# A hybrid attention and convolution layer on one core: two helper constants built later, one weight tile loaded alone, and sums over partitions merged per head

## The chip, the core and the metric

The kernel runs on one core of one Trainium2 chip. The metric is the device time of one execution in microseconds (us), as the median of several runs; lower is better. Before the change the median of 3 runs is 643.99 us (642.95 to 644.54).

## What is computed

One layer with batch 1, 1024 positions and width 1024, all in float32:

```python
h = rms_norm(x, pre_norm_gain)
q, k, v, z_a, b_gate, c_gate, u, z_c = split(h @ w_in, 8)
# group A: 4 heads, two softmax maps each, block-causal mask, ALiBi
attn = (softmax(q0 k0' + bias) - lam * softmax(q1 k1' + bias)) @ v
attn = rms_norm(attn, subln_gain, 1e-5) * 0.2 * silu(z_a)
# group B: gated depthwise convolution of width 3
conv_out = b_gate * conv3(c_gate * u) * silu(z_c)
x = x + rms_norm(concat(attn, conv_out) @ w_out, post_norm_gain)
e = rms_norm(p @ w_ple_proj, ple_norm_gain)
out = x + sigmoid(x @ w_ple_gate) * e
```

## The kernel before

Everything stands transposed: features on the 128 partitions, positions along the row, in two halves of 512 (`n` = 0, 1). Every product is split into three matmuls (`mm3`, L99 to L102), since each float32 operand is held as a high part and a low part: L100 is high by high, L101 high by low, L102 low by high. The high part is a cast on ACT, the low part a subtraction on DVE or, for most weights, on POOL (`split`, L87 to L93). In the names, `pth`/`pto` are high and low part of p, `wph`/`wpo` those of `w_ple_proj`, `hT` those of x, `w` those of a weight tile.

The stages in order of time:

- **Start (0 to about 42 us).** Nine idle matmuls (L347), then the embedding p @ w_ple_proj (`embed`, L330 to L340): 8 tiles of 6 matmuls for each half. Its weights come in three loads into buffers of the pool `rawp`, which has three (`load_ple`, L303 to L318): tile 0 on ACT's queue (128 KB), tiles 1 to 3 with a table of small constants (402.5 KB), tiles 4 to 7 (512 KB), both on SP's queue; p comes in quarters (`load_p`, L320 to L328), x in 16 tiles (`load_x`, L298). DVE also builds two helpers out of the identity here (L170 to L172): `fold`, 128 by 128, in four reductions, and `own`, 128 by 4, in one. All later sums over partitions use them.
- **Projections.** `run` (L144) makes q, k and z of head 0, then v for all heads (L401), with the weights `wv`, whose four tiles are loaded at L395 and split on ACT and DVE.
- **Heads.** `PLAN` (L31) lists the steps of each head: softmax tiles (`a`), values (`g0`, `g1` for the halves, L256), convolution tiles to keep PE busy (`c`, 48 matmuls each), scaling the values by their norms (`n0`, `n1`, `scale_values` L283), and the embedding's norms (`s0`, `s1`, `embed_scale` L447).
- **Output.** The product with `w_out`, its norm, the product with `w_gate`, stores.

A sum of squares over partitions is `column_sums` (L105): DVE transposes 32 by 32 blocks (`flip`), reduces (`part`), PE multiplies by `fold` (a single matmul `ms`, L116, into a bank of 512), then `rsqrt` (L95) makes a scale on DVE and takes the power -0.5 on POOL (L97, 128 by 16), with the exponent from the constant `nhalf`. `values` does this once for each half of each head, with 16 columns of sums and 16 of softmax sums (`extra`, through `own`), `embed_scale` once for each half, and x and the output twice each: 14 `ms` matmuls and 14 powers in all.

The order of instructions on each engine is not written by hand. The program is scheduled as a whole by a timing model when it is built, so a change in one place can move rows in others; an engine then works through its rows strictly in that order, and SP's queue does so with the loads.

Of the kernel before, what the change touches and what calls it, by code (L numbers as in the profile page):

```python
# [43 lines left out]
def hybrid_layer(ctx, tc, xT, pT, w_in, lams, w_out, w_ple, w_gate, outT):  # L44
# [14 lines left out]
    small_c = edge.tile([P, 96], F32, name="small_c")  # L59
# [16 lines left out]
    nhalf = small_c[:, 4:20]  # L76
# [10 lines left out]
    def split(hi, lo, src, scale=None, lo_eng=None):  # L87
        if scale is None:
            A.copy(out=hi, in_=src)  # L89
            (lo_eng or V).tensor_tensor(out=lo, in0=src, in1=hi.bitcast(F32), op=sub)  # L90
# [14 lines left out]
    def column_sums(acc, pool, extra=None, tag="flip"):  # L105
        flip = pool.tile([P, HALF], F32, tag=tag, name="flip")
        V.transpose(out=flip, in_=acc)
        part = tiny.tile([P, 32], F32, tag="part", name="part")
        V.tensor_reduce(out=part[:, 0:16], in_=flip.rearrange("p (f r) -> p f r", r=32), axis=AX.X, op=add)
        if extra is not None:  # L110
            V.tensor_tensor(out=part[:, 16:32].rearrange("p (t f) -> p t f", t=4),
                            in0=extra.unsqueeze(2).broadcast_to([P, 4, 4]),
                            in1=own.unsqueeze(1).broadcast_to([P, 4, 4]), op=mult)
        n = 16 if extra is None else 32
        ms = bank_t("ms")
        T.matmul(out=ms[:, :n], lhsT=fold, rhs=part[:, :n], start=True, stop=True)  # L116
        return ms

# [33 lines left out]
    r_col = const.tile([P, NT + 80], F32, name="r_col")[:, :NT]  # L152
    R = [const.tile([P, HALF], F32, name=f"R{n}") for n in range(2)]

    with ExitStack() as st:
# [14 lines left out]
        for g in range(4):  # L170
            V.tensor_reduce(out=fold[:, 32 * g:32 * g + 32], in_=ident.rearrange("p (a b) -> p b a", a=4), axis=AX.X, op=add)
        V.tensor_reduce(out=own, in_=ident.rearrange("p (f r) -> p f r", r=32), axis=AX.X, op=add)  # L172

        class Head:
            def __init__(s, h):
# [12 lines left out]
                s.rs = {}  # L188
# [67 lines left out]
            def values(s, g):  # L256
# [16 lines left out]
                ms = column_sums(sq, ap, extra=r0)  # L273
                rb = tiny.tile([P, 16], F32, tag="rb", name="rb")
                rs = tiny.tile([P, 16], F32, tag="rs", name="rs")
                V.tensor_copy(out=rb, in_=ms[:, 16:32])
                V.tensor_tensor(out=rs, in0=ms[:, 0:16], in1=rb, op=mult)
# [3 lines left out]
                s.rs[g] = rs  # L281
# [8 lines left out]
        with ExitStack() as st0:  # L290
# [13 lines left out]
            def load_ple(c, o, queue=nc.sync, constants=0):  # L304
# [6 lines left out]
                cuts = [0, 1, c.stop - c.start] if constants else [0, c.stop - c.start]  # L311
                for a, b in zip(cuts, cuts[1:]):
                    w = slice(c.start + a, c.start + b)
                    if c.start == 0:
                        V.tensor_copy(out=wph[:, w], in_=raw[:, a:b])
                        V.tensor_tensor(out=wpo[:, w], in0=raw[:, a:b], in1=wph[:, w].bitcast(F32), op=sub)
                    else:
                        split(wph[:, w], wpo[:, w], raw[:, a:b])  # L318

            def load_p(n):  # L320
                pth = s2.tile([P, 2, HALF], F32R, tag="pth", name="pth")
                pto = s2.tile([P, 2, HALF], F32R, tag="pto", name="pto")
                raw = p_raw[:, n].bitcast(F32).rearrange("p (k a) b -> p k (a b)", k=2)
                for k in range(2):
                    nc.sync.dma_start(out=raw[:, k], in_=pT[:, n, k])
                    split(pth[:, k], pto[:, k], raw[:, k])
                return pth, pto

            def embed(n, p):
                pth, pto = p  # L330
# [20 lines left out]
            load_ple(slice(1, 4), 256, constants=37)  # L351
            load_ple(slice(4, 8), 1024 + 37)
            embed(0, pt0)
# [11 lines left out]
        with ExitStack() as st0:  # L365
# [81 lines left out]
        def embed_scale(n):  # L447
# [23 lines left out]
        for h in range(H):  # L471
# [5 lines left out]
            for step in PLAN[h]:  # L477
# [21 lines left out]
    with ExitStack() as st:  # L499
# [40 lines left out]
        def post_stat(n):  # L540
            r = tiny.tile([P, 16], F32, tag="rs", name="rso")
            rsqrt(r, column_sums(accs[n], cp)[:, :16], D, 1e-6)
# [90 lines left out]
```

## Time and profile before

| | before |
|---|---|
| median of 3 runs | 643.99 us |
| profiled execution, its own time | 643.39 us |
| its span, first to last instruction | 641.6 us |
| PE busy | 632.6 us, 99% |
| DVE busy | 447.9 us, 70% |
| ACT busy | 242.3 us, 38% |
| POOL busy | 227.6 us, 35% |
| mean granted TensorE clock | 0.996 |

PE is TensorE's matmuls, DVE the vector engine, ACT the scalar engine, POOL GpSimd, SP the engine that issues most loads and stores. A row of a timeline gives start and duration in us, the engine, the line of the kernel, what is written from what, and in brackets how long the engine stood idle before it and on whom it waited. Matmuls overlap in the pipeline: a matmul of 512 columns is listed with 0.39 us, but the next one starts 0.227 us later, so the pace of PE is read from the starts. The profiled execution lies 0.60 us under the median and inside the spread of the three runs.

### The profile page before, as it was taken

How to read it: one execution, taken by the hardware profiler on the slowest of the kernel's cores; microseconds unless marked ns; L12 is line 12 of the kernel's file. 1: busy time of each engine (PE TensorE's matmuls, PEld its weight loads, DVE VectorE, ACT ScalarE, POOL GpSimd, SP SyncE). 2: the span in 40 equal slices, each digit the busy share in tenths (PEclk: the TensorE clock that was granted, in tenths of full speed). 3: DMA queues.
4: the chain of work that ended last, by engine and by line, in shares of the span. 5: the costliest groups of instructions: out<-in, count | busy, mean ns of one | idle time of the engine just before them, and what ended most of it. 6: DMA issues, size and time to landing. Idle time of an engine off the chain costs nothing.

```text
span 641.6 us, 8064 instructions
## 1 busy us (share of the span) xinstructions
PE 632.6 (99%) x2941; PEld 524.8 (82%) x2941; DVE 447.9 (70%) x824; ACT 242.3 (38%) x442; POOL 227.6 (35%) x114
## 2 busy tenths in 40 slices
PE   8999999999999999999999999999999999999997
PEld 4888788888888888887888888888888888888886
DVE  6977612688786688776886999628993179898342
ACT  5936312334454333553343533322732225413111
POOL 2013300324326636237461142433760087741000
PEclk8999999999999999999999999999999999999999
DMA  8976612210244112353113411111360034124231
GB/s 301 391 268 161 228 78 102 88 39 27 83 130 149 50 33 59 85 170 97 36 33 90 127 46 34 42 55 36 119 242 33 2 98 150 64 84 146 84 114 50
DMA packets 35511, 67.78 MB, mean 106 GB/s; under 512 B 3600, under 2 KB 12304, under 8 KB 35472
## 3 DMA queue, kind: packets, MB, share of 16 engines
q1 hardware_dynamic: 35328, 67.14, 31.6%
q8 instruction: 23, 0.38, 0.2%
q10 hardware_dynamic: 144, 0.13, 0.1%
q14 instruction: 16, 0.13, 0.1%
HBM read 48.38 MB, written 12.58 MB: 95 GB/s over the span
## 4 chain that ended last, share of the span: by engine, by line
PE 89%; DVE 4%; DMA 3%; POOL 2%; ACT 1%; issue 1%; POOLq 0%; DVEq 0%; ACTq 0%
PE pj L100 13%; PE pj L102 13%; PE pj L101 13%; PE o L102 9%; PE o L100 9%; PE o L101 9%; PE s L237 5%; PE tpw L264 2%; PE v L100 2%; PE v L102 2%; PE v L101 2%; PE av L102 1%; PE ple L101 1%; PE av L101 1%; POOL mix L455 1%; PE av L100 1%
## 5 line engine op out<-in xcount | busy, mean ns | idle before, releaser
L100 PE MATMUL pj<-hT,w 128*128 128x512 f32 x448 | 176.3, 394 | 0.0
L101 PE MATMUL pj<-hT,w 128*128 128x512 f32 x448 | 176.2, 393 | 0.0
L102 PE MATMUL pj<-hT,w 128*128 128x512 f32 x448 | 176.2, 393 | 0.0
L90 POOL TENSOR_TENSOR w<-raw,w 128x1024 fp32r<-128x1024 f32 x41 | 105.6, 2581 | 145.1 <-ACT w L89 145.1
L102 PEld LDWEIGHTS pj<-hT,w 128*128 128x128 f32 x448 | 84.2, 188 | 16.4
L101 PEld LDWEIGHTS pj<-hT,w 128*128 128x128 f32 x448 | 84.2, 188 | 16.2
L100 PEld LDWEIGHTS pj<-hT,w 128*128 128x128 f32 x448 | 84.2, 188 | 16.1
L245 ACT ACTIVATE p<-p,nm 128x128 f32<-128x128 f32 (+7 forms) x64 | 49.4, 772 | 70.6 <-DVE nm L241 60.7
L89 ACT CAST w<-raw 128x1024 fp32r<-128x1024 f32 x44 | 45.8, 1047 | 19.4 <-issue 11.0
L102 PE MATMUL o<-x,w 128*128 128x512 f32 (+1 forms) x136 | 51.3, 377 | 0.0
L100 PE MATMUL o<-x,w 128*128 128x512 f32 (+1 forms) x136 | 51.2, 377 | 0.0
L101 PE MATMUL o<-x,w 128*128 128x512 f32 (+1 forms) x136 | 51.2, 377 | 0.0
L100 PE MATMUL o<-mT,w 128*128 128x512 f32 x128 | 49.8, 389 | 0.0
L101 PE MATMUL o<-mT,w 128*128 128x512 f32 x128 | 49.8, 389 | 0.0
L102 PE MATMUL o<-mT,w 128*128 128x512 f32 x128 | 49.7, 390 | 0.0
L237 PE MATMUL s<-ks,qs 128*128 128x512 f32 (+2 forms) x192 | 47.5, 346 | 0.5 <-ACT w L89 0.5
L89 ACT CAST wt<-tpw 128x512 fp32r<-128x512 f32 (+3 forms) x48 | 21.1, 479 | 60.2 <-PE tpw L264 60.2
L90 DVE TENSOR_TENSOR wt<-tpw,wt 128x512 fp32r<-128x512 f32 (+3 forms) x48 | 25.3, 550 | 26.3 <-ACT wt L89 26.2
L241 DVE CUSTOM_DVE_ANT_0 p<-s,bias 128x512 f32<-128x512 f32 (+3 forms) x64 | 34.8, 564 | 9.4 <-PE s L237 5.4
L237 PEld LDWEIGHTS s<-ks,qs 128*128 128x128 f32 x192 | 33.3, 188 | 5.8 <-ACT w L89 0.8
L418 POOL TENSOR_TENSOR mix<-mix,R 128x512 f32<-128x512 f32 x8 | 12.3, 1542 | 66.1 <-DVE mix L417 64.0
L253 DVE SCALAR_TENSOR_TENSOR p<-p,rl,p 128x128 f32<-128x128 f32 (+7 forms) x32 | 32.7, 1021 | 0.4
(142 smaller groups left out, 1101.6 us busy)
## 6 DMA issues: line engine op xcount, KB each, us to landing
raw<-in_w_in SPq DMA_DIRECT2D x32, 512.0 KB, 3.4
mix<-in_xT SPq DMA_DIRECT2D x16, 256.0 KB, 5.5
e_dram<-e SPq DMA_DIRECT2D x16, 256.0 KB, 6.0
mix<-e_dram SPq DMA_DIRECT2D x16, 256.0 KB, 3.0
ks<-ks SPq DMA_DIRECT2D x16, 256.0 KB, 3.6
v_dram<-v SPq DMA_DIRECT2D x8, 512.0 KB, 2.6
vs<-v_dram SPq DMA_DIRECT2D x32, 128.0 KB, 2.7
raw<-in_w_out SPq DMA_DIRECT2D x8, 512.0 KB, 3.3
```

The source lines that it names most:

```text
L89: A.copy(out=hi, in_=src)
L90: (lo_eng or V).tensor_tensor(out=lo, in0=src, in1=hi.bitcast(F32), op=sub)
L100: T.matmul(out=ps, lhsT=ah, rhs=bh, start=first, stop=False)
L101: T.matmul(out=ps, lhsT=ah, rhs=bl, start=False, stop=False)
L102: T.matmul(out=ps, lhsT=al, rhs=bh, start=False, stop=last)
L237: T.matmul(out=banks[m][:, :nn], lhsT=s.qs[:, m, qi], rhs=s.ks[:, m, part, c], start=part == 0, stop=part == 1)
L241: V.tensor_tensor_reduce(out=pr[m][:, c0:c0 + n], in0=banks[m][:, :n], in1=s.bias[:, b0:b0 + n], scale=-1.0, scalar=low[m], op0=add, op1=A ...
L245: A.activation(out=pr[m][:, :W], in_=pr[m][:, :W], func=AF.Exp, scale=-1.0, bias=low[m], accum_out=l[:, m:m + 1])
L253: V.scalar_tensor_tensor(out=pr[0][:, :W], in0=pr[1][:, :W], scalar=rl, in1=pr[0][:, :W], op0=mult, op1=add)
L264: T.transpose(out=tp[:, ii * P:(ii + 1) * P], in_=s.ws[ii][:, j * P:(j + 1) * P], identity=ident)
L418: G.tensor_tensor(out=o, in0=o, in1=R[n], op=mult)
L455: G.tensor_tensor(out=acc, in0=acc, in1=e, op=add)
```

## The change

Four things are changed. The five reductions that build `fold` and `own` are issued after the last low part of p's first half, not before. The load of tiles 1 to 3 is cut: tile 1 comes alone (128 KB) and is cast on DVE in place of ACT; tiles 2 and 3 come with the constants (274.5 KB). In each head, both halves put their sums into one tile of 64 columns, and a new step `r` (`row_scales`) makes one `ms` matmul, one chain of small DVE operations and one power of 32 columns, where each half had its own. The embedding's two halves likewise share one `ms` and one power of 32 columns, made in the second half's call. There are 9 `ms` matmuls and 9 powers now.

```diff
-    ['a0123', 'v', 'g0', 'a4567', 'g1', 'c1', 'n0', 'c1', 's0', 'n1', 'c1'],
+    ['a0123', 'v', 'g0', 'a4567', 'g1', 'c1', 'r', 'n0', 'c1', 's', 'n1', 'c1'],
...
-    def column_sums(acc, pool, extra=None, tag="flip"):
+    def partial(part, acc, pool, tag="flip"):
         flip = pool.tile([P, HALF], F32, tag=tag, name="flip")
         V.transpose(out=flip, in_=acc)
...
+        V.tensor_reduce(out=part, in_=flip.rearrange("p (f r) -> p f r", r=32), axis=AX.X, op=add)
+
+    def total(part):
+        ms = bank_t("ms")[:, :part.shape[-1]]
+        T.matmul(out=ms, lhsT=fold, rhs=part, start=True, stop=True)
         return ms
...
-        for g in range(4):
-            V.tensor_reduce(out=fold[:, 32 * g:32 * g + 32], in_=ident.rearrange("p (a b) -> p b a", a=4), axis=AX.X, op=add)
-        V.tensor_reduce(out=own, in_=ident.rearrange("p (f r) -> p f r", r=32), axis=AX.X, op=add)
...
-                ms = column_sums(sq, ap, extra=r0)
...
+                if g == 0:
+                    s.part = tiny.tile([P, 64], F32, tag="part4", name="part4")
+                c = slice(16 * g, 16 * g + 16)
+                partial(s.part[:, c], sq, ap)
...
+            def row_scales(s):
+                ms = total(s.part)
+                rb = tiny.tile([P, 32], F32, tag="rb", name="rb")
+                rs = tiny.tile([P, 32], F32, tag="rs", name="rs")
+                V.tensor_copy(out=rb, in_=ms[:, 32:64])
+                V.tensor_tensor(out=rs, in0=ms[:, 0:32], in1=rb, op=mult)
                 V.tensor_tensor(out=rs, in0=rs, in1=rb, op=mult)
                 rsqrt(rs, rs, P, 1e-5)
                 V.tensor_tensor(out=rs, in0=rs, in1=rb, op=mult)
-                s.rs[g] = rs
+                s.rs = [rs[:, 0:16], rs[:, 16:32]]
...
+                if c.start < 2:
+                    V.tensor_copy(out=wph[:, c], in_=raw)
+                    V.tensor_tensor(out=wpo[:, c], in0=raw, in1=wph[:, c].bitcast(F32), op=sub)
+                else:
+                    split(wph[:, c], wpo[:, c], raw)
...
             pt0 = load_p(0)
-            load_ple(slice(1, 4), 256, constants=37)
+            load_ple(slice(1, 2), 256)
+            load_ple(slice(2, 4), 512, constants=37)
             load_ple(slice(4, 8), 1024 + 37)
+            with tc.issue_after(pt0[2][1].ins):
+                for g in range(4):
...
-            r = rs_e[:, 16 * n:16 * n + 16]
-            rsqrt(r, column_sums(acc, ap)[:, :16], D, 1e-6)
-            V.tensor_scalar(out=r, in0=r, scalar1=0.5, scalar2=None, op0=mult)
+            partial(rs_e[:, 16 * n:16 * n + 16], acc, ap)
+            if n:
+                rsqrt(rs_e, total(rs_e), D, 1e-6)
+                V.tensor_scalar(out=rs_e, in0=rs_e, scalar1=0.5, scalar2=None, op0=mult)
```

The schedule moves in three places of which the prediction speaks. The first is DVE's queue at the start; `rawe` is a raw weight tile, `p_raw` a quarter of p. Before:

```order
L315 CAST wph<-rawe 128x256
L171 TENSOR_REDUCE fold<-ident 128x32 x4
L172 TENSOR_REDUCE small_c<-ident 128x4
L316 TENSOR_TENSOR wpo<-rawe,wph 128x256
L90 TENSOR_TENSOR pto<-p_raw,pth 128x512 x2
L309 COPY small_c<-rawe 128x37
L90 TENSOR_TENSOR wpo<-rawe,wph 128x256
L90 TENSOR_TENSOR wpo<-rawe,wph 128x512
```

Now:

```order
L317 CAST wph<-rawe 128x256
L90 TENSOR_TENSOR pto<-p_raw,pth 128x512
L318 TENSOR_TENSOR wpo<-rawe,wph 128x256
L317 CAST wph<-rawe 128x256
L90 TENSOR_TENSOR pto<-p_raw,pth 128x512
L358 TENSOR_REDUCE fold<-ident 128x32 x2
L318 TENSOR_TENSOR wpo<-rawe,wph 128x256
L358 TENSOR_REDUCE fold<-ident 128x32 x2
L360 TENSOR_REDUCE small_c<-ident 128x4
L314 COPY small_c<-rawe 128x37
L90 TENSOR_TENSOR wpo<-rawe,wph 128x512
```

The five reductions have gone behind both low parts of p and are spread round the second tile's low part.

The second place is SP's queue of loads at the start (`mix<-in_xT` is a tile of x). Before:

```order
L325 DMA p_raw<-in_pT 128x512 x2
L307 DMA rawe<-in_w_ple 128x805
L307 DMA rawe<-in_w_ple 128x1024
L301 DMA mix_0_110<-in_xT 128x512
L301 DMA mix_0_112<-in_xT 128x512
L301 DMA mix_0_114<-in_xT 128x512
L301 DMA mix_0_116<-in_xT 128x512
```

Now:

```order
L327 DMA p_raw<-in_pT 128x512 x2
L312 DMA rawe<-in_w_ple 128x256
L312 DMA rawe<-in_w_ple 128x549
L306 DMA mix_0_110<-in_xT 128x512
L306 DMA mix_0_112<-in_xT 128x512
L306 DMA mix_0_114<-in_xT 128x512
L312 DMA rawe<-in_w_ple 128x1024
L306 DMA mix_0_116<-in_xT 128x512
```

Tiles 4 to 7 are now the fourth load into a pool of three buffers; they stand behind three tiles of x and wait until the first tile's buffer is free.

The third place is DVE's queue after the first half's norm of x is known (`R0`), where head 0's q and k (`tq`, `ql`, `tk`) and the weights of v (`wv`) are split. Before:

```order
L194 SCALAR_TENSOR_TENSOR tq_532<-pj_507,R0_128 128x512
L90 TENSOR_TENSOR ql_533<-tq_532,qs_428 64x512
L203 TENSOR_TENSOR tk_566<-pj_541,R0_128 128x512
L90 TENSOR_TENSOR ql_533<-tq_532,qs_428 64x512
L96 TENSOR_SCALAR rsx_471<-ms_498 128x16
L90 TENSOR_TENSOR wv_704<-raw_705,wv_704 128x8x128
L90 TENSOR_TENSOR wv_704<-raw_709,wv_704 128x8x128
L90 TENSOR_TENSOR wv_704<-raw_713,wv_704 128x8x128
```

Now:

```order
L190 SCALAR_TENSOR_TENSOR tq_534<-pj_509,R0_128 128x512
L90 TENSOR_TENSOR wv_706<-raw_707,wv_706 128x8x128
L96 TENSOR_SCALAR rsx_473<-ms_500 128x16
L90 TENSOR_TENSOR wv_706<-raw_711,wv_706 128x8x128
L90 TENSOR_TENSOR wv_706<-raw_715,wv_706 128x8x128
L90 TENSOR_TENSOR ql_535<-tq_534,qs_430 64x512
L199 TENSOR_TENSOR tk_568<-pj_543,R0_128 128x512
L90 TENSOR_TENSOR ql_535<-tq_534,qs_430 64x512
```

The splits of `wv`, which free the raw buffers for the next weights, now come before `ql` and `tk`.

## Rows read from the trace of the kernel before

**Rows 1.** Waits of PE, whole span: engine and line, releaser; us in total, times, longest.
```profile
PE ms L116 <- DVE part L109: 0.5, 1, 0.5
PE s L237 <- ACT w L89: 0.5, 1, 0.5
PE v L100 <- DVE mix L216: 0.4, 1, 0.4
```

**Rows 2.** Timeline of PE at the start: start us, us, instruction, idle before it.
```profile
5.52 0.50 PE L100 MATMUL ple<-pth,wph 128*128 128x512 f32 x1 [0.40 <-ACT pth L89]
7.61 0.50 PE L101 MATMUL ple<-pto,wph 128*128 128x512 f32 x1 [1.59 <-DVE pto L90]
...
9.06 0.63 PE L101 MATMUL ple<-pto,wph 128*128 128x512 f32 x1
9.49 0.63 PE L100 MATMUL ple<-pth,wph 128*128 128x512 f32 x1
...
14.68 0.39 PE L100 MATMUL ple<-pth,wph 128*128 128x512 f32 x1
```

**Rows 3.** Windows: stretch, its length, busy per engine (count), PE clock, DMA share, GB/s.
```profile
8.00:12.10 4.10, 4.10 (x12) 3.06 (x11) 3.05 (x8) 3.78 (x6) 0.00 (x0) 0.58 1.05 405
...
20.00:42.00 22.00, 22.00 (x99) 18.22 (x98) 20.25 (x35) 18.23 (x32) 0.00 (x0) 1.00 0.96 365
```

**Rows 4.** Timeline of DVE at the start.
```profile
5.01 0.29 DVE L315 CAST wph<-rawe 128x256 fp32r<-128x256 f32 x1 [3.90 <-DMA rawe<-in_w_ple]
5.22 1.21 DVE L171 TENSOR_REDUCE fold<-ident 128x32 f32<-128x128 f32 x4
...
6.87 1.37 DVE L90 TENSOR_TENSOR pto<-p_raw,pth 128x512 fp32r<-128x512 f32 x2
...
10.32 1.23 DVE L90 TENSOR_TENSOR wpo<-rawe,wph 128x1024 fp32r<-128x1024 f32 x1 [0.22 <-ACT wph L89]
...
15.97 1.29 DVE L90 TENSOR_TENSOR pto<-p_raw,pth 128x512 fp32r<-128x512 f32 x2
```

**Rows 5.** Timeline of ACT at the start.
```profile
6.89 0.62 ACT L89 CAST pth<-p_raw 128x512 fp32r<-128x512 f32 x1 [1.43 <-DMA p_raw<-in_pT]
...
9.24 1.05 ACT L89 CAST wph<-rawe 128x1024 fp32r<-128x1024 f32 x1 [0.31 <-DMA rawe<-in_w_ple]
```

**Rows 6.** The tile `rawe`: us from a load's issue to its landing (three loads).
```profile
DMA to landing us min/median/max: 4.3/6.3/7.1
```

**Rows 7.** Timeline of SP: the first four loads of x.
```profile
2.58 2.75 SPq L301 DMA_DIRECT2D mix<-in_xT  x4
```

**Rows 8.** Timeline of PE round its three later stops.
```profile
63.91 0.39 PE L102 MATMUL pj<-hT,w 128*128 128x512 f32 x1
64.75 0.48 PE L237 MATMUL s<-ks,qs 128*128 128x256 f32 x2 [0.45 <-ACT w L89]
...
70.28 0.39 PE L102 MATMUL v<-wv,hT 128*128 128x512 f32 x1
71.04 0.50 PE L100 MATMUL v<-wv,hT 128*128 128x512 f32 x1 [0.38 <-DVE mix L216]
...
302.53 0.39 PE L101 MATMUL pj<-hT,w 128*128 128x512 f32 x1
303.41 0.40 PE L116 MATMUL ms<-part,fold 128*128 128x16 f32 x2 [0.49 <-DVE part L109]
```

**Rows 9.** The chain of waits between 40 and 72 us: start us, us, what.
```profile
53.61 2.39 DVE wv L90 x2
56.01 7.35 DMA raw<-in_w_in
```

**Rows 10.** Timeline of PE round one `ms` matmul; two rows lie between.
```profile
513.30 0.39 PE L101 MATMUL o<-mT,w 128*128 128x512 f32 x1
...
513.98 0.40 PE L100 MATMUL o<-mT,w 128*128 128x512 f32 x1
```

**Rows 11.** Line L97, the power on POOL in the heads: duration ns min/median/max.
```profile
L97 POOL TENSOR_TENSOR rs<-rs,small_c x8: 2900/2920/3274, 154.4 to 448.8; 128x16 f32<-128x16 f32 x8
```

More of the change, by code (lines that the diff above doesn't have):

```diff
@@ L88, in split @@
         if scale is None:
-            A.copy(out=hi, in_=src)
-            (lo_eng or V).tensor_tensor(out=lo, in0=src, in1=hi.bitcast(F32), op=sub)
+            return (A.copy(out=hi, in_=src),
+                    (lo_eng or V).tensor_tensor(out=lo, in0=src, in1=hi.bitcast(F32), op=sub))
         else:
@@ L102, in mm3, with column_sums @@
         T.matmul(out=ps, lhsT=al, rhs=bh, start=False, stop=last)
-    def column_sums(acc, pool, extra=None, tag="flip"):
+    def partial(part, acc, pool, tag="flip"):
         flip = pool.tile([P, HALF], F32, tag=tag, name="flip")
         V.transpose(out=flip, in_=acc)
[L108 to L116, printed above, removed]
-        return ms
+        V.tensor_reduce(out=part, in_=flip.rearrange("p (f r) -> p f r", r=32), axis=AX.X, op=add)
+    def total(part):
+        ms = bank_t("ms")[:, :part.shape[-1]]
+        T.matmul(out=ms, lhsT=fold, rhs=part, start=True, stop=True)
+        return ms
+    def column_sums(acc, pool, tag="flip"):
+        part = tiny.tile([P, 16], F32, tag="part", name="part")
+        partial(part, acc, pool, tag)
+        return total(part)
     def spread(out, row):
@@ L151, in hybrid_layer @@
     gt = const.tile([P, HALF + 2], F32, name="gt")
[L152 removed]
+    r_col = const.tile([P, NT + 96], F32, name="r_col")[:, :NT]
     R = [const.tile([P, HALF], F32, name=f"R{n}") for n in range(2)]
@@ L272, in values @@
                 V.tensor_tensor(out=o, in0=av, in1=o, op=mult)
-                ms = column_sums(sq, ap, extra=r0)
[L274 to L277, printed above, removed]
+                if g == 0:
+                    s.part = tiny.tile([P, 64], F32, tag="part4", name="part4")
+                c = slice(16 * g, 16 * g + 16)
+                partial(s.part[:, c], sq, ap)
+                V.tensor_tensor(out=s.part[:, 32 + 16 * g:48 + 16 * g].rearrange("p (t f) -> p t f", t=4),
+                                in0=r0.unsqueeze(2).broadcast_to([P, 4, 4]),
+                                in1=own.unsqueeze(1).broadcast_to([P, 4, 4]), op=mult)
+            def row_scales(s):
[4 more added lines that the diff above has]
+                V.tensor_tensor(out=rs, in0=ms[:, 0:32], in1=rb, op=mult)
                 V.tensor_tensor(out=rs, in0=rs, in1=rb, op=mult)
@@ L310, in load_ple @@
                 raw = raw[:, :n].rearrange("p (a b c) -> p a b c", b=2, c=P)
[L311 to L318, printed above, removed]
+                if c.start < 2:
[3 more added lines that the diff above has]
+                    split(wph[:, c], wpo[:, c], raw)
             def load_p(n):
@@ L325, in load_p @@
                     nc.sync.dma_start(out=raw[:, k], in_=pT[:, n, k])
-                    split(pth[:, k], pto[:, k], raw[:, k])
-                return pth, pto
+                    last = split(pth[:, k], pto[:, k], raw[:, k])
+                return pth, pto, last
             def embed(n, p):
-                pth, pto = p
+                pth, pto, _ = p
                 for m in range(KT):
@@ L350, in hybrid_layer @@
             pt0 = load_p(0)
-            load_ple(slice(1, 4), 256, constants=37)
+            load_ple(slice(1, 2), 256)
+            load_ple(slice(2, 4), 512, constants=37)
             load_ple(slice(4, 8), 1024 + 37)
+            with tc.issue_after(pt0[2][1].ins):
+                for g in range(4):
+                    V.tensor_reduce(out=fold[:, 32 * g:32 * g + 32], in_=ident.rearrange("p (a b) -> p b a", a=4),
+                                    axis=AX.X, op=add)
+                V.tensor_reduce(out=own, in_=ident.rearrange("p (f r) -> p f r", r=32), axis=AX.X, op=add)
             embed(0, pt0)
@@ L540, in post_stat @@
         def post_stat(n):
-            r = tiny.tile([P, 16], F32, tag="rs", name="rso")
-            rsqrt(r, column_sums(accs[n], cp)[:, :16], D, 1e-6)
+            r = tiny.tile([P, 32], F32, tag="rs", name="rso")[:, :16]
+            rsqrt(r, column_sums(accs[n], cp), D, 1e-6)
             return r
```

13 lines of the change are left out of this document (7 added, 6 removed), and 6 rows, old and new, of the table PLAN.

## Prediction

> **What bounds the kernel now.** I read the table of busy time first: PE works 99% of the span, so a change counts only if it takes matmuls off PE, lets PE start its work earlier, or ends a stop of PE. Then the waits of PE: behind the start there are three, each once, and together they are small [rows 1]. The reader is to see there that no other wait is left between 72 us and the end. The size of each stop is better read from the starts of matmuls, against the usual step of 0.23 us [rows 8]: 63.91 to 64.75 loses 0.61 us, 70.28 to 71.04 loses 0.53, 302.53 to 303.41 loses 0.65, in sum 1.79 us. Last, the start [rows 2]: PE stands for 1.59 us before its second matmul at 7.61, then steps at 0.43 us (9.06 to 9.49), which is the lower of TensorE's two levels (1.2 GHz of 2.4), with a mean grant of 0.58 from 8.0 to 12.1 us [rows 3]. The matmul at 14.68 is the 25th of the embedding, counted in the timeline.
>
> Measured from no change, 0.3% is 1.9 us, about what a measurement of this kernel can tell. The sum below is made against the profiled execution's own 643.39 us (span 641.6); the median of the runs shown is 0.60 higher, within their spread.
>
> **The change, part by part.**
>
> *Reductions moved.* Before, DVE builds the copies for 1.21 us from 5.22 [rows 4], and p's low part, for which L101 waits, comes only at 7.6. Now the low part of the first quarter starts when its high part is there, at 5.5 (when L100 ran), takes 0.69 (half of 1.37 for two), and L101 runs near 6.3. The gain is not the 1.3 us between, since the next matmul needs the second quarter, whose cast ends at 6.89 + 0.62 = 7.51 [rows 5]. From 7.55 on PE has work for a while.
>
> *Tile 1 alone.* It costs one more issue on SP, 0.4 us, and moves a cast from ACT to DVE, 0.29 us by the cast of tile 0 [rows 4]. I put its landing near 7.2: issued at 1.6 like the first `rawe` load there, and between the ends 4.3 and 7.1 us [rows 6], so 5.9 to 8.7; a fifth of a megabyte less than what went at that place should be on the early side of the middle. It is then just there when PE asks.
>
> *Tiles 4 to 7 late.* They now wait for a raw buffer, free after tile 0's low part, near 6.6 (5.3 end of the cast, 5.5 to 6.2 p's low part, 0.4). Landing 4.3, 6.3 or 7.1 us later [rows 6] is 10.9, 12.9 or 13.7; with the cast of 1.05 [rows 5], 12.0, 14.0 or 14.8. In the changed order 24 matmuls stand ahead of the first that needs it, the 25th. Those 24 would be done at 14.0 if the lower clock comes again as before (8 steps of 0.43 from 8.3 to 11.75, the others at 0.23), and at 12.5 if it doesn't. So the 25th starts at 14.0 with the middle landing, against 14.68: **0.7 us** gained. The ends: 0.1 us lost with the last landing (14.8), which I widen to 0.35 for a queue on ACT, where three splits of x stand ahead of the cast; and 1.2 gained if the load is early and the clock stays. The 34th matmul then needs the low part of tiles 4 to 7, 1.23 us on DVE [rows 4] and behind those splits of x, near 15.5; before, PE was there at 14.68 + 9 x 0.23 = 16.7. So 1.2 is all there is. DVE's reductions themselves are still made, and their cover is the wait for loads.
>
> *Chain from 42 to 71 us.* The stop at 64.75 follows on ACT's cast of a weight, that on a load that took 7.35 us from 56.01, and that on two splits of `wv`, 2.39 us from 53.61, which free its buffer [rows 9]. The changed order puts these splits ahead of `ql` and `tk`, so the load can go some 3 to 4 us earlier; and the score matmuls, which stood at 64.75, are moved behind a whole tile of v. The stop at 71.04 is the end of the same chain (DVE waits for ACT, which waits for the cast). What is late next is q and k themselves, behind three splits of 1.2 us; the z of the second half, which frees a bank, comes near 67.1 by these durations, and PE asks for it 24 steps after the first tile of v, about 68.7. I take both stops as ended, **0.61 + 0.53 us**; the other end is that they stay.
>
> *Embedding sums.* The stop at 303.41 waits for the reduction behind the second half's sum. In the changed order its matmul stands 31.4 us of PE work behind the head's last value product, before 26.1 (rows of the order times their steps). The sum came 26.8 us after it. A power of 32 columns in POOL's queue between may take up to twice 2.92 us [rows 11], which makes it 29.8. Still early: **0.65 us** gained, other end nothing.
>
> *Five `ms` matmuls fewer.* 513.30 to 513.98 is 0.68 us for two matmuls and one `ms` [rows 10], where two steps take 0.454, so one costs 0.23. Five are **1.13 us**; they lie on PE's path, so I take all of it. That one with 64 columns costs more is bounded by the 0.23 of a whole step with 512.
>
> *Five powers and their chains fewer.* A power of 16 columns takes 2.92 us [rows 11]; one of 32 takes between the same (a fixed cost) and 5.8. Nothing on PE waits for one in the heads before. In heads 0 to 2 the scaled values are used only in the output product, so cost and gain there are nothing. In head 3 the scaling of both halves now hangs on the second half's sums, in front of the output product. I followed DVE's rows: after `ms`, 1.6 us to the power, 2.9 to 5.8 for it, then the wait for the product of b (32 steps, 7.3 us after `ms`), nine operations of about 0.7, and the bank PE needs is free 14 to 16 us after `ms`; PE comes to it after 85 steps, 19.4 us. 3 to 5 us are spare: nothing, with an end in the rivals.
>
> *The new order itself.* It moves rows on every engine, and I have read it closely at these places only. A drawn order of this program stops PE for 1.79 us [rows 8]; the places I read are free now, so I put half of that, **0.9 us**, for stops elsewhere; ends 0 and 1.79.
>
> Sum: -0.7 - 0.61 - 0.53 - 0.65 - 1.13 + 0.9 = -2.72; 643.39 - 2.72 = **640.7 us**. With all best ends -1.2 - 1.79 - 1.13 = -4.12, 639.3; with all worst +0.35 - 1.13 = -0.78, 642.6.
>
> **The rivals.**
>
> *The clock stays up at the start.* The lower level came right after PE's idle 1.59 us [rows 2, 3]. That idle time is now cut in two, about 0.5 and 0.7 us, so the lower stretch may come later, shorter or not at all. For it: more work before 8.3 us. Against: the wait for tiles 4 to 7 then becomes the stop, about 1.5 us long, and the clock may fall behind it in its turn. The Trainium skill ("TensorE: Matmul & The Clock Gate", Part 1) says that the throttled state is the default and that activity releases it; by that, a busier PE would keep the high level, and the trace agrees so far that the idle came before the fall. With it the start gives 1.2, and with no new stops this is 639.3. Chance 0.14.
>
> *Stops only change place.* The order is drawn anew, and PE stops as long elsewhere. Then -0.7 - 1.13 = -1.83: 641.6. For it: DVE is busy 20.3 of 22 us from 20 to 42 [rows 3], so small shifts can tell. Chance 0.20.
>
> *The start gives nothing and the stops remain.* Only the five matmuls are won: 642.3. Chance 0.08.
>
> *Slower: the load stream.* SP stands at tiles 4 to 7 until 6.6; the fourth x, which was issued near 4.9 (the last of four from 2.58 over 2.75 us [rows 7]), goes near 7.0, and all loads behind it 2.1 us later. The DMA engines are busy for 0.96 of the time to 42 us [rows 3], so the lost time may not be made up. If p's second half or x then come late, PE is 2.1 us later at 42, and with the stops still there 643.39 + 2.1 - 1.13 = 644.4. It decides when the delay exceeds what is spare: p's second half is split by 15.97 + 1.29 = 17.3 [rows 4], and PE asks for it after 48 matmuls, near 14.68 + 23 x 0.23 = 19.9, so 2.6 us are spare, a little more than 2.1. Chance 0.08. The Trainium skill ("DMA: Bandwidth & Descriptors", Bandwidth) gives the rule to batch loads to 1 MiB or more, which speaks against cutting the load of tiles 1 to 3; the rows agree that a smaller load is not proportionally faster (4.3 us for 128 KB, 7.1 for 512) [rows 6], but the loads run beside each other, and only a bound stream would turn the rule into time, as in this rival.
>
> **How the numbers follow.** The forecast has 0.50, the rivals 0.14, 0.20, 0.08 and 0.08. Faster by over 0.3% means a median under 642.06: all of the first rival, nearly all of the forecast (0.49), 0.12 of the second: 0.75. Slower by over 0.3%, above 645.92, takes the load stream with a further stop: 0.04. The rest, 0.21, is no change. For 8 in 10, the range goes down to 638.9 (the best ends, less the half microsecond by which a median can lie off a single execution) and up to 642.8 (the worst ends of the sum); it leaves out most of the last rival and the edges of the others.
>
> **What would show it.** Right: L101 of the first tile near 6.3 us; the 25th embedding matmul near 14.0; no stop of PE at the score matmuls, at the second tile of v, nor at the embedding's `ms`; 9 `ms` matmuls, so 18 records where there were 28; PE's new stops together under 1 us. A power of 32 columns tells whether 2.9 or 5.8 holds. Wrong: a 25th matmul after 14.7 (late load), a second stretch at the lower clock, stops at p's second half near 20 us, a stop before the second tile of the output product, or stops of over 2 us elsewhere.

## The result: slower, where faster was forecast

| | before | after |
|---|---|---|
| median, range, runs on the same chip | 643.23 us (642.56 to 644.67), 20 | 647.07 us (644.29 to 651.96), 20 |
| ratio, 95% interval | | 1.0067 [1.0049, 1.0086] |
| profiled execution, its own time | 643.39 us | 651.96 us |
| its span; mean granted clock | 641.6 us; 0.996 | 649.7 us; 0.992 |

The profiled execution of after is the slowest of its 20: eight of them had a mean granted clock of 0.999 or 1.000 and took 644.29 to 646.41 us, the other twelve had 0.992 to 0.997 and took 646.35 to 651.96, so the profile shows the stops, and the lower clock behind them, at their worst. From here on a time in us against before is the ratio's distance from 1 times 643.2: after costs +4.3 us.

### The profile page after: what moved, and what is told of

Read it like the earlier page. It is cut to its first block, busy times and chain, and to the rows that moved or that the text cites. A ratio compares the mean times of both kernels' runs of the same rounds, so it can differ in the third digit from the quotient of the medians.

```text
span 649.7 us, 8008 instructions
## 1 busy us (share of the span) xinstructions
PE 636.1 (98%) x2931; PEld 525.4 (81%) x2931; DVE 445.5 (69%) x803; ACT 242.4 (37%) x441; POOL 222.5 (34%) x109
## 4 chain that ended last, share of the span: by engine, by line
PE 92%; DVE 3%; DMA 1%; ACT 1%; SPq 1%; issue 1%; ACTq 0%
PE pj L101 15%; PE pj L102 15%; PE pj L100 15%; PE o L100 9%; PE o L101 8%; PE o L102 8%; PE s L233 5%; PE tpw L260 2%; PE v L101 2%; PE v L102 2%; PE v L100 2%; PE av L101 1%; PE av L102 1%; DVE mT L90 1%; PE av L100 1%; PE ple L100 1%
## 5 line engine op out<-in xcount | busy, mean ns | idle before, releaser
L101 PE MATMUL pj<-hT,w 128*128 128x512 f32 x448 | 177.6, 397 | 0.0
L90 POOL TENSOR_TENSOR w<-raw,w 128x1024 fp32r<-128x1024 f32 x41 | 104.7, 2560 | 159.5 <-ACT w L89 156.5
L101 PEld LDWEIGHTS pj<-hT,w 128*128 128x128 f32 x448 | 84.9, 190 | 16.4
L100 PE MATMUL o<-mT,w 128*128 128x512 f32 x128 | 50.4, 395 | 2.5 <-DVE mix L453 2.5
L101 PE MATMUL o<-x,w 128*128 128x512 f32 (+1 forms) x136 | 51.2, 377 | 0.0
L102 PE MATMUL o<-mT,w 128*128 128x512 f32 x128 | 50.4, 394 | 0.0
L101 PE MATMUL o<-mT,w 128*128 128x512 f32 x128 | 50.1, 393 | 0.0
L237 DVE CUSTOM_DVE_ANT_0 p<-s,bias 128x512 f32<-128x512 f32 (+3 forms) x64 | 34.7, 564 | 9.5 <-PE s L233 5.5
L90 DVE TENSOR_TENSOR wt<-tpw,wt 128x512 fp32r<-128x512 f32 (+3 forms) x48 | 25.1, 551 | 22.0 <-ACT wt L89 21.9
L426 POOL TENSOR_TENSOR mix<-mix,R 128x512 f32<-128x512 f32 x8 | 10.8, 1345 | 70.6 <-DVE mix L425 70.6
L584 ACT ACTIVATE tg<-o 128x512 f32<-128x512 f32 (+1 forms) x17 | 9.7, 572 | 57.1 <-PE o L102 53.3
```

The lines of the kernel that those rows point to most:

```text
L100: T.matmul(out=ps, lhsT=ah, rhs=bh, start=first, stop=False)
L101: T.matmul(out=ps, lhsT=ah, rhs=bl, start=False, stop=False)
L102: T.matmul(out=ps, lhsT=al, rhs=bh, start=False, stop=last)
L237: V.tensor_tensor_reduce(out=pr[m][:, c0:c0 + n], in0=banks[m][:, :n], in1=s.bias[:, b0:b0 + n], scale=-1.0, scalar=low[m], op0=add, op1=A ...
L426: G.tensor_tensor(out=o, in0=o, in1=R[n], op=mult)
L584: A.activation(out=t, in_=ps, func=AF.Tanh, scale=0.5)
```

## The profile after

The waits of PE over the whole span (columns as in [rows 1]):

```profile
PE s L233 <- issue: 3.6, 1, 3.6
PE o L100 <- DVE mix L453: 2.5, 1, 2.5
...
PE tpw L260 <- DVE rs L282: 0.8, 1, 0.8
PE av L101 <- DVE wt L90: 0.6, 1, 0.6
```

None of the three waits of [rows 1] is left; four others stand in their place, all of them longer. The start did better than forecast. The timeline of PE there:

```profile
5.30 0.48 PE L100 MATMUL ple<-pth,wph 128*128 128x512 f32 x1
6.01 0.51 PE L101 MATMUL ple<-pto,wph 128*128 128x512 f32 x1 [0.23 <-DVE pto L90]
...
12.24 0.50 PE L100 MATMUL ple<-pth,wph 128*128 128x512 f32 x1 [0.22 <-ACT wph L89]
...
14.68 0.40 PE L102 MATMUL ple<-pth,wpo 128*128 128x512 f32 x1
```

L101 runs at 6.01 where it ran at 7.61 [rows 2], and the 25th matmul, at 12.24, stood at 14.68 before. The row at 14.68 is the 34th. The later stops, in the same view:

```profile
200.35 0.39 PE L101 MATMUL pj<-hT,w 128*128 128x512 f32 x1
201.57 0.41 PE L260 MATMUL tpw<-ident,p 128*128 128x128 f32 x2 [0.84 <-DVE rs L282]
...
288.44 0.39 PE L100 MATMUL pj<-hT,w 128*128 128x512 f32 x1
292.47 0.77 PE L233 MATMUL s<-ks,qs 128*128 128x256 f32 x2 [3.65 <-issue]
293.04 0.63 PE L101 MATMUL pj<-hT,w 128*128 128x512 f32 x1
293.47 0.63 PE L102 MATMUL pj<-hT,w 128*128 128x512 f32 x1
...
477.02 0.39 PE L102 MATMUL o<-mT,w 128*128 128x512 f32 x1
479.88 0.77 PE L100 MATMUL o<-mT,w 128*128 128x512 f32 x1 [2.47 <-DVE mix L453]
```

The first of these is the stop at 200, the second that at 288, the third that at 477; less one step they last 1.0, 3.8 and 2.6 us. Behind the two long ones PE steps at 0.43 us: the stop is paid a second time, as the windows show (columns as in [rows 3]):

```profile
0.00:20.00 20.00, 18.26 (x66) 11.64 (x67) 15.20 (x34) 13.71 (x22) 4.45 (x9) 1.00 0.90 299
...
288.00:292.40 4.40, 0.83 (x4) 0.36 (x2) 4.37 (x6) 0.25 (x1) 3.27 (x3) 0.93 0.31 119
292.40:298.60 6.20, 6.13 (x16) 4.90 (x17) 4.81 (x10) 1.56 (x3) 0.00 (x0) 0.50 0.01 3
```

At the start the clock stays at 1.00; from 292.4 it is 0.50 (1.2 GHz) for 6.2 us, which costs half of that, some 3 us, behind a stop of 3.8. The Trainium skill ("TensorE: Matmul & The Clock Gate", HAM oscillation) says that work after a wait can start throttled again and that this transition is paid at every such wait; the trace agrees in these two places. It isn't so behind every stop, and the length alone does not decide it: behind one of 2.3 us in e12 and one of 2.0 in e9 (kernels described below) the clock stayed at 1.00, behind one of 2.1 us in e1 and those of 2.0 us in e11 and e13 it fell.

Where the time went, from the starts of all matmuls: each distance less the undisturbed step (0.227 us for 512 columns, less for shorter ones), summed by stretch. Some 3 us in each of the stretches 150-290 and 290-440 are in every kernel and are no stops (short matmuls, whose steps I set by hand); a row is to be read against another, not by itself. The kernels e1 to e14 are described in the next section.

| lost in the profiled run, us | 0-42 | 42-75 | 75-150 | 150-290 | 290-440 | 440-520 |
|---|---|---|---|---|---|---|
| before | 5.98 | 1.50 | 0.55 | 2.91 | 4.10 | 0.09 |
| after | 3.94 | 0.15 | 0.68 | 5.03 | 10.22 | 4.27 |
| e2, start alone | 4.26 | 0.15 | 0.60 | 2.86 | 3.88 | 0.08 |
| e1, after with short powers | 4.36 | 0.15 | 0.68 | 4.08 | 7.14 | 1.13 |
| e11, embedding's first sum kept | 4.35 | 0.15 | 0.68 | 3.51 | 3.36 | 4.56 |
| e12, head 3 by halves | 4.20 | 0.15 | 0.68 | 4.53 | 6.41 | 0.83 |
| e13, e11 with short powers | 4.24 | 0.15 | 0.68 | 2.72 | 3.08 | 4.58 |
| e14, both of these undone | 4.03 | 0.15 | 0.68 | 3.27 | 3.84 | 0.08 |

After less before is -2.04 - 1.35 + 0.13 + 2.12 + 6.12 + 4.18 = +9.16; five `ms` less, -1.13: +8.0, and the spans differ by 8.1. So the gain at the start and up to 75 us is 3.4, and more is lost from 150 us on.

## Experiments

Times are medians, with the range, the number of runs, and the ratio to before on the same chip.

**The powers.** A power of 32 columns takes 5.4 us, [rows 11] has 2.92 for 16. The timeline of POOL in after, in head 3:

```profile
451.15 5.42 POOL L97 TENSOR_TENSOR rs<-rs,small_c 128x32 f32<-128x32 f32 x1 [0.34 <-DVE rs L96]
462.59 14.18 POOL L90 TENSOR_TENSOR w<-raw,w 128x1024 fp32r<-128x1024 f32 x5 [6.03 <-ACT w L89]
```

and that of DVE there:

```profile
456.60 0.19 DVE L285 TENSOR_TENSOR rs<-rs,rb 128x32 f32<-128x32 f32 x1 [1.74 <-POOL rs L97]
```

e1 keeps the order of after on every engine and makes the five long powers short: once the order is drawn, a product (0.24 us) is put in the place of each.

```diff
-        G.tensor_tensor(out=out, in0=out, in1=nhalf[:, :ssq.shape[-1]], op=ALU.pow)
+        pows.append(G.tensor_tensor(out=out, in0=out, in1=nhalf[:, :ssq.shape[-1]], op=ALU.pow).ins.name)
...
+    swap = set(pows[2:7])
+    for f in nc.m.functions:
+        for b in f.blocks:
+            for k, i in enumerate(b.instructions):
+                if i.name in swap:
+                    b.instructions[k] = copy.replace(i, op=ALU.mult)
```

> The changed kernel with every engine's order untouched; only the operation of the five powers of 32 columns (four heads, embedding) is made a product, so the heads' and the embedding's scales are other numbers. Theory A (the power of 32 columns takes 5.4 us, twice that of 16, and DVE's next row stands for it): the stops of PE near 288 and 477 us go, those near 200 to 204 (1.9 us) stay, 640 to 642 us, and runs lie within 2 us of each other. Theory B (the new order is to blame, whatever the power takes): the stops stay, 645 to 651. Theory C (late loads of the embedding, ahead of POOL's additions): the stop at 288 stays, that at 477 goes, 644 to 647.

Measured: 643.70 us (642.67 to 645.98, 12), 1.0020 [1.0007, 1.0033]. So the length of the powers is worth 3.0 us, in after's order. But 1.3 us over before remain, and in its trace stops at 200 (0.5 us), 288 (2.1, in place of 3.8) and 473 us (0.9, in place of 2.6): the theory of the powers holds only in part, and the time lies between its bracket and those of the others.

**The parts alone.** e2 has the reductions moved and tile 1 cut off; e3 has the merged sums of the heads; e4 has the embedding's.

> Kernel before with the start alone changed (helpers later, second weight tile alone). The 25th embedding matmul near 12.2 us and the lower clock absent, as in the profile after. Theory A: the gain of 2.4 us at the start stays to the end, 640 to 642 us. Theory B: the order is drawn anew behind it too, so stops appear elsewhere, 643 to 647.

> Kernel before with the heads' sums, chain and power merged (step r), start and embedding as before. Theory A: 4 ms matmuls less (0.9 us), but stops behind the long power, 645 to 650 us and a wide spread. Theory B: anything between 642 and 650, with stops at other places than behind the power. Theory C: 642 to 643, since the embedding's own sums are as before.

> Kernel before with the embedding's sums and power merged alone. Theory A: one ms matmul less and the stop at 303 us gone or moved, 642 to 643.5 us. Theory B: 642 to 647. Theory C: stops of 2 us or more where the embedding's additions run, 645 to 648.

Measured: e2 640.48 us (640.17 to 641.25, 5), 0.9965 [0.9953, 0.9977]; e3 650.16 (649.61 to 650.71, 4), 1.0113 [1.0099, 1.0128]; e4 652.12 (651.54 to 653.51, 4), 1.0146 [1.0133, 1.0159]. The start is worth 2.3 us by itself, and the stops at 64.75 and 71.04 are gone with it alone. The embedding's merged sum, one matmul and one power fewer, costs 9.4 us, more than any theory had it. By the count recorded before e5, 462 of PE's rows stand at other places in the program's order than before, and PE's waits in e4 show stops that were not there:

```profile
PE pj L100 <- DVE mix L451: 3.1, 1, 3.1
PE tpw L265 <- DVE p L254: 1.9, 3, 1.2
PE s L238 <- DVE nm L242: 1.9, 2, 1.0
```

**Which half of the embedding's edit.** e5 is e4 with the long power, but each half keeps its own `ms`; PE's order is then that of before but for four rows. e8 is the start and e4 together.

```diff
-            partial(rs_e[:, 16 * n:16 * n + 16], acc, ap)
+            r = rs_e[:, 16 * n:16 * n + 16]
+            partial(r, acc, ap)
+            V.tensor_scalar(out=r, in0=total(r), scalar1=1.0 / D, scalar2=1e-6, op0=mult, op1=add)
             if n:
-                rsqrt(rs_e, total(rs_e), D, 1e-6)
+                G.tensor_tensor(out=rs_e, in0=rs_e, in1=nhalf, op=ALU.pow)
```

> As e4 (embedding alone), but the first half's sum over partitions keeps its own ms matmul in head 0; the power of 32 columns for both halves stays in head 1. With this matmul back, PE's order is that of the kernel before but for 4 rows (462 differ in e4). Theory D (the matmul's bank, one of the two that the transposes of the value products use too, held these transposes behind the filler products; without it the order leaves softmax uncovered): 642 to 644 us. Theory A (the power of 5.4 us): 649 to 652 as in e4.

> Start and embedding changed, heads as before. If the parts add up, e4's 652.1 less the 2.5 of e2: 649 to 650 us (theory A and D). Theory B, that each order is a draw of its own: anything between 640 and 652, most likely not within 1 us of 649.6.

Measured: e5 642.95 us (641.52 to 644.26, 12), 0.9987 [0.9974, 1.0000]; e8 649.79 (649.10 to 650.95, 6), 1.0101 [1.0084, 1.0118]. The power of 5.4 us is in e5 and costs nothing there: it is the missing first `ms` that costs 10.2 us (e4 against e5), and e8 keeps that cost beside the start's gain. The traces of before and e5 have the same matmuls in the same places but for four, so the cost comes with the other order that is drawn without it.

**Heads 0 to 2, and a step of PE that changed.** e6 and e7 merge the sums of heads 0 to 2 only, e7 with the start.

> As e3 (heads merged, start and embedding as before), but head 3 keeps a sum, a chain and a power of 16 columns for each half. Theory E (at the seam to the output product the first half's scale waits for the second half's sum and the long power; ACT's casts of mT, behind them the casts of the output weights, behind them POOL's splits come late): the stop near 470 us goes, 642 to 645 us. Theory B (redrawn order anywhere): 647 to 650 as in e3.

> e6 with the changed start as in e2. Theory E: the sum of both, 639.5 to 642 us, at or below e2's 640.5, since three ms matmuls are gone (0.7 us). Theory B: 645 to 648.

Measured: e6 648.82 us (647.16 to 650.00, 6), 1.0087 [1.0066, 1.0108]; e7 645.72 (645.35 to 646.69, 8), 1.0040 [1.0027, 1.0053]. Both lie in the brackets of theory B, but not by its stops: behind the start, e7 has none of note and e6 two of 0.7 and 0.8 us. They are slow all the same: PE is busy all the time at a granted clock of 1.00 and gets less done. My edits had moved operands of matmuls in SBUF to 128 (e6, e7) or 192 (e3) bytes behind a multiple of 256. So e3 and e7 were repeated, with the order of every engine unchanged, as e9 and e10, where an unused stretch behind the scales brings the operands back to multiples of 256:

```diff
-    r_col = const.tile([P, NT + 80], F32, name="r_col")[:, :NT]
+    r_col = const.tile([P, NT + 112], F32, name="r_col")[:, :NT]
```

(e10; in e9 it is `NT + 96`, as in the changed kernel.)

> As e3 (heads merged alone), same order on every engine, but with 64 bytes of padding that put the operands of the matmuls back on multiples of 256 bytes, where they lie in the kernels before and after and where e3 had moved them (to 192 over one). Theory F (off these multiples a matmul step takes 228 to 232 ns in place of 226.7, as read from e3, e6 and e7): 644 to 646.5 us, with the stop near 470 us still there. Rival: the step is set by something else, 649 to 651 as in e3.

> As e7 (start, heads 0 to 2 merged, head 3 and embedding as before), padded in the same way. Theory F: 639 to 640.8 us, e2's 640.5 less up to 0.7 for three ms matmuls. Theory B (the heads' new order stops PE elsewhere): 642 to 646.

Measured: e9 647.41 us (644.77 to 647.75, 6), 1.0059 [1.0046, 1.0071]; e10 641.00 (639.52 to 641.74, 5), 0.9958 [0.9946, 0.9971]. Both lie between the brackets of theory F and of its rival. The address was worth 4.7 us between the medians of e7 and e10 (5.3 by the ratios). Windows of PE alone, first of e7:

```profile
520.00:560.00 40.00, 40.00 (x176) 1.00 0.34 112
560.00:600.00 40.00, 40.00 (x175) 1.00 0.34 106
```

and of e10:

```profile
520.00:560.00 40.00, 40.00 (x179) 1.00 0.35 106
560.00:600.00 40.00, 40.00 (x179) 1.00 0.36 112
```

The same matmuls, one after the other: 351 against 358 in the same 80 us, 2% fewer. The mean distance of their starts there is 0.2307 us against 0.2267. It isn't so for every product: in e7 the product `v<-wv,hT` (0.233) and both output products `o` (0.231) step slower than in e10, the fillers `pj<-hT,w` keep their 0.227. The slower steps of `v` and `o` (188 and 737 of them) add up to 4.1 us. So the times of e3 and e6 say nothing on the merged sums; e9 and e10 do. Heads 0 to 2 cost nothing, and what costs is in head 3: e9 loses 3.0 us between 440 and 520 us, before 0.1, with a stop of 2.0 us at 468.

**The two places in the changed kernel.** e11 is the changed kernel with the embedding's first `ms` kept (the diff of e5), e12 the changed kernel with the two halves of head 3 summed and scaled apart, as before.

> The changed kernel, but the embedding's first half keeps its own ms matmul in head 0. Theory D (that matmul's bank held the transposes behind the filler): the stops near 200 and 288 us go, the one at the seam to the output product stays, 642 to 644.5 us. Rival: those stops come from the heads' merged sums, 646 to 648.

> The changed kernel, but head 3 keeps a sum and a power for each half. Theory E (the seam: both halves' scales wait for the second sum and the long power, then ACT's casts, then POOL's splits): the stop near 477 us goes, those near 200 and 288 stay, 643 to 645.5 us. Rival (theory D alone, the seam is late because the order before it is): 646 to 649.

Measured: e11 644.46 us (642.40 to 645.43, 12), 1.0015 [1.0004, 1.0027]; e12 646.65 (644.59 to 649.00, 7), 1.0046 [1.0028, 1.0065]. Undoing the embedding's sum gives back 3.3 us of 4.3, undoing head 3 only 1.3. In e11 the stops at 200 and 288 us are gone, in e12 that at 477, each as expected; but e12's time lies in its rival's bracket, so head 3 is worth less while the other two stops stand.

How one missing sum stops PE is seen at head 1. The timelines of DVE and POOL in after:

```profile
198.49 2.84 DVE L214 SCALAR_TENSOR_TENSOR mix<-tz,mix 128x512 f32<-128x512 f32 x1 [2.77 <-ACT tz L213]
201.25 0.18 DVE L282 TENSOR_TENSOR rs<-ms,rb 128x32 f32<-128x32 f32 x1
...
198.38 2.40 POOL L90 TENSOR_TENSOR w<-raw,w 128x1024 fp32r<-128x1024 f32 x1
```

and the same operations of DVE in e11:

```profile
198.74 2.84 DVE L214 SCALAR_TENSOR_TENSOR mix<-tz,mix 128x512 f32<-128x512 f32 x1 [3.10 <-ACT tz L213]
201.50 0.18 DVE L282 TENSOR_TENSOR rs<-ms,rb 128x32 f32<-128x32 f32 x1
```

DVE reads the head's `ms` out at 201.25 in the one and at 201.50 in the other: equally late, since L214 stands ahead of it and waits for ACT, and ACT for a load of the embedding (`mix<-e_dram`, 3.71 us of idle time before 194.64); then L214 takes 2.84 us beside POOL's split, where the one at 190.50 took 0.79. In after the next thing on PE that needs the bank is a transpose of p (`tpw`), which takes turns with `ms` in the same two banks; it is asked for at 200.6 and starts at 201.57. In e11 no transpose stands there: some 41 matmuls of fillers (`pj`) and scores run from 195.21 to 204.66. The embedding's first sum was one turn in this ring of two banks. Without it the order has the transposes ahead of the fillers, where they wait for whatever is late. That it is this turn, and not something else in the model that draws the order, is argued from the two orders: no run keeps the sum out of the ring and the rest as it was.

The stop at 288 comes with the missing sum too (e11 has none there, e12 has), but by another bank. ACT stood 5.00 us for an embedding load up to 282.83, with the exponentials queued behind it, and DVE was late after that. The profile names no releaser, but the score matmul starts 0.10 us after DVE's L237 has read a bank of scores, and in e12 and e1 the score matmul behind the stop starts 0.1 us after the same operation. Ahead of that row DVE is slow beside POOL's split and additions. DVE and POOL in after:

```profile
286.30 2.17 DVE L248 SCALAR_TENSOR_TENSOR rl<-rl,l,small_c 128x1 f32<-128x1 f32 x1
288.50 1.72 DVE L249 SCALAR_TENSOR_TENSOR p<-p,rl,p 128x512 f32<-128x512 f32 x1
...
291.82 0.55 DVE L237 CUSTOM_DVE_ANT_0 p<-s,bias 128x384 f32<-128x384 f32 x1
...
286.02 2.43 POOL L90 TENSOR_TENSOR w<-raw,w 128x1024 fp32r<-128x1024 f32 x1 [1.13 <-ACT w L89]
288.40 2.94 POOL L463 TENSOR_TENSOR mix<-mix,mix 128x512 f32<-128x512 f32 x2
```

and in e12, where the split starts later and the stop is 2.3 us, not 3.8:

```profile
286.33 0.22 DVE L249 SCALAR_TENSOR_TENSOR rl<-rl,l,small_c 128x1 f32<-128x1 f32 x1
286.58 0.75 DVE L250 SCALAR_TENSOR_TENSOR p<-p,rl,p 128x512 f32<-128x512 f32 x1
...
290.05 0.54 DVE L238 CUSTOM_DVE_ANT_0 p<-s,bias 128x384 f32<-128x384 f32 x1
...
287.08 2.49 POOL L90 TENSOR_TENSOR w<-raw,w 128x1024 fp32r<-128x1024 f32 x1 [0.99 <-ACT w L89]
```

The stop at 477 is drawn out in the same way. PE waits for L453, and ahead of it DVE has five operations beside POOL's split of the output weight, from 464.96 to 477.25; at their usual pace they would end some 9 us earlier (an estimate from the rows of 0.7 us):

```profile
474.45 2.88 DVE L449 SCALAR_TENSOR_TENSOR mix<-ty,mix 128x512 f32<-128x512 f32 x1
...
479.05 0.68 DVE L453 TENSOR_TENSOR mix<-pj,mix 128x512 f32<-128x512 f32 x1
```

The slowing itself is not new: the kernel before has it in head 3 as well, and no stop of PE there.

```profile
461.06 2.90 DVE L90 TENSOR_TENSOR mT<-mix,mT 128x512 fp32r<-128x512 f32 x1
```

By these rows the new order decides where PE has no time to spare, and POOL's work beside DVE adds to how long it then stands. No run moves POOL's splits alone, so their share isn't shown by an experiment.

**What is left in head 3.** e11 still stops for 2.0 us at 465.72 and has the lower clock behind it (0.60 on the mean from 468 to 472). e13 is e11 in the same order with short powers, as in e1.

> The changed kernel with the first half's sum of the embedding kept, as in e11 (644.46 us; stop of PE from 465.72 to 467.97, where the second tile of the output weight's low part comes late from POOL), in the same order on all engines, with a product in place of the power in the four heads and in the embedding (the scales are then other numbers). Theory F (what is left in head 3 is the place of the work: ACT's casts of mT for both halves stand in front of its casts of the output weight, and what released DVE's chain there was PE's product at 453.2 us, not the power, which was over at 452.8): the stop stays, at 1.5 us or more, and the time is 643.5 to 644.8. Theory G (the power's 5.4 us is what makes it late): the stop falls under 0.7 us and the time is 640 to 642.

> Start, sums of heads 0 to 2 and the single power of the embedding as in the changed kernel; the embedding's sum of the first half and the two sums of head 3 as in the kernel before; operands at multiples of 256 bytes. If the two places found (embedding's first sum, head 3) are all that costs time, all of the gain at the start and of three sums is kept and nothing is lost: 639.5 to 641.2, like e10 (641.00), and below e2 (640.48) by at most 0.7. If the long powers or the merged sums of heads 0 to 2 cost time of their own: 642 or more.

Measured: e13 643.15 us (641.39 to 643.74, 12), 0.9995 [0.9984, 1.0005]. The stop is the same, in e11's timeline of PE

```profile
465.72 0.39 PE L101 MATMUL o<-mT,w 128*128 128x512 f32 x1
467.97 0.50 PE L102 MATMUL o<-mT,w 128*128 128x512 f32 x1 [1.86 <-POOL w L90]
```

and in e13's:

```profile
466.79 0.50 PE L106 MATMUL o<-mT,w 128*128 128x512 f32 x1 [1.87 <-POOL w L94]
```

though the power took 0.24 us in place of 5.42. What makes it late is in e13's timelines of DVE, ACT and POOL:

```profile
452.05 0.69 DVE L449 TENSOR_TENSOR y<-pj,R 128x512 f32<-128x512 f32 x1 [4.76 <-PE pj L106]
452.65 0.18 DVE L289 TENSOR_TENSOR rs<-rs,rb 128x32 f32<-128x32 f32 x1
...
454.94 6.35 ACT L93 CAST mT<-mix 128x512 fp32r<-128x512 f32 x12 [1.48 <-DVE mix L296]
461.20 2.94 ACT L93 CAST w<-raw 128x1024 fp32r<-128x1024 f32 x3
...
462.32 12.82 POOL L94 TENSOR_TENSOR w<-raw,w 128x1024 fp32r<-128x1024 f32 x4 [15.86 <-ACT w L93]
```

DVE stands 4.76 us for PE's filler, whose row is ahead of the scaling in its queue; then twelve casts of `mT` stand on ACT ahead of the casts of the output weight, and POOL splits that weight behind them. As expected by theory F the stop stays, and the time lies 0.4 us under its bracket, above that of theory G. What the short powers gain in e13, 1.3 us, is not at this stop; by the table above it is 0.8 between 150 and 290 us and 0.3 behind.

e14: 639.67 us (639.37 to 640.48, 6), 0.9945 [0.9933, 0.9957], the fastest of all kernels here, and faster than before and after. In its timeline of ACT the output weight's casts come after the first casts of `mT`, not after all:

```profile
454.66 1.98 ACT L89 CAST mT<-mix 128x512 fp32r<-128x512 f32 x3
457.88 1.14 ACT L89 CAST mT<-mix 128x512 fp32r<-128x512 f32 x2 [1.23 <-DVE mix L312]
458.93 2.94 ACT L89 CAST w<-raw 128x1024 fp32r<-128x1024 f32 x3
```

Against before, step by step: start -2.3 (e2); with heads 0 to 2, -2.7 (e10); with one power for the embedding, -3.5 (e14); with head 3 merged, +1.0 (e11); without the embedding's first sum, +4.3 (after). Undone in this order, head 3 costs 4.5 us and the sum 3.3; with the sum taken away first (e14 to e12) the sum costs 6.5 and head 3 (e12 to after) 1.3, so the two overlap.

## Why the prediction was wrong

By its own steps:

- *Start* (forecast -0.7). Right in the way, too small. The 25th matmul came at 12.24, ahead of the best end, and the clock stayed at 1.00: this part of the first rival, given 0.14, is what happened. The bound of 1.2 us failed too: the 34th, put near 15.5, ran at 14.68, where it ran at 16.72 before. Start and chain to 71 us give 2.04 + 1.35 = 3.4 us in the profiled run; e2 measures 2.3 in the median.
- *Chain from 42 to 71 us* (-0.61 - 0.53). Right: 1.50 lost before, 0.15 after, in e2 as well.
- *Five `ms` fewer* (-1.13). Not shown by itself. e10 and e14 against e2 give 0.4 and 1.3 us with three fewer, each known to 0.8 or so (e14 has the merged power of the embedding as well); nothing contradicts 0.23 for one.
- *Embedding sums* (-0.65). This is a step that failed. The stop at 303.41 went, as forecast, but the step looked only at the matmul that waits. It did not ask what order would be drawn without the sum that was removed, which takes turns in two banks with the transposes. Removing it cost 3.3 us in the changed kernel (after against e11) and 10.2 alone (e4 against e5); with the sum kept and the power merged the time fell by 0.8 (e5), hardly more than the noise.
- *Five powers and their chains fewer* (0). This failed too. Its upper end for the power was right, 5.4 us; that nothing on PE waits for one in heads 0 to 2 is right as well in the order with the sum kept (e10, e14). In head 3 the step followed DVE to the bank that PE needs, and found 3 to 5 us to spare, but it did not follow ACT: the merged scaling lets twelve casts come at once, ahead of the output weight's. That costs 4.5 us (e14 to e11), and e13 shows that the power's length has no part in that stop. In the changed kernel's own order it has: there DVE does stand for the power in head 3, and with short powers (e1) the time is 3.0 us less and the last stop 0.9 us, not 2.6.
- *The new order itself* (+0.9, ends 0 to 1.79). The size failed. I bounded it by the stops of one drawn order, as though every order were equally good. The new one lost 2.12 + 6.12 + 4.18 us more than the old from 150 us on in the profiled run, a third of it through the lower clock behind two stops (some 3 us and 1.4). Nor did the sum of the worst ends hold this term's own worst end: with 1.79 it is +1.01, not -0.78, and ends at 644.4. The measured median lies above that as well.

Of the rivals, "stops only change place" has the right mechanism, with a wrong price: it took the new stops to be as long as the old. Among the signs of being wrong, stops of over 2 us elsewhere came, and a second stretch at the lower clock. The rival that ended slower, the load stream, did not occur: the sum of lost time between 20 and 42 us is -0.03 in both kernels.

What stays open: how long each of the stops at 200, 288 and 477 us lasts in a median run of after, since only its slowest was profiled; how much of them is POOL's work beside DVE; and whether it is the turn in the ring that makes the order, as argued at head 1.

## What to carry to other kernels

Before a small operation is merged away, look at which ring of buffers it takes a turn in and who else does: where a program draws the order, one turn less can let others be moved ahead to where they wait. When two halves of a chain are merged, follow every engine's queue behind the merge, not only the one that ends at the busiest engine: what came in two portions now comes in one, ahead of something else. Where a queue has two-input work on DVE, look at what POOL does beside it. And test the parts of such a change apart: here a start worth 2.3 us was hidden under sums that cost more.

## What the runs showed of the hardware

The step of matmuls of 512 columns depends on where their operands lie in SBUF: 0.2267 us in the output product with the buffers at multiples of 256 bytes, 0.231 at 128 and 0.228 at 192 bytes behind one (e7 to e10, e3 to e9, at a clock of 1.00); for `v`, 0.227 against 0.233 in both. The fillers `pj<-hT,w` of the same kernels keep 0.227, so it isn't PE's pace as a whole; which operand of a product decides was not tried. The Trainium skill ("SBUF — State Buffer", Operand start alignment) asks only for a multiple of the element's size and says that its runs timed nothing; these runs add the time. The changed kernel's own edit of `r_col`, from `NT + 80` to `NT + 96`, keeps its operands at multiples of 256; I had left that line out of account.

The power's time on POOL grows with its columns, 2.92 to 5.42 us for 16 and 32. DVE goes on at its usual pace beside it, but not beside POOL's splits and additions, which adds to the stops above; DVE's timeline in after:

```profile
452.97 0.68 DVE L90 TENSOR_TENSOR mT<-mix,mT 128x512 fp32r<-128x512 f32 x1
...
463.19 0.69 DVE L445 TENSOR_TENSOR y<-pj,R 128x512 f32<-128x512 f32 x1
...
471.64 2.88 DVE L90 TENSOR_TENSOR mT<-mix,mT 128x512 fp32r<-128x512 f32 x1
```

The first runs beside the power, the other two beside the splits. The Trainium skill ("GPSIMD Engine Reference", Specifications) says that GpSimd shares its SBUF interfaces with VectorE and that the two contend where a DVE operation has two SBUF inputs. The trace agrees for the splits: L90 with two such inputs takes four times as long, L445, which reads PE's bank, does not. It shows no such effect of the power, which also reads two inputs but takes 5.4 us for 32 columns.
